# Opening, end and twelve chunks of filling work moved in a one-core encoder block kernel

## The chip, the core and the metric

The kernel runs on one core of one Trainium2 chip. The metric is the device time of one execution in microseconds (us), lower is better. Three executions of the kernel before took 1316.39, 1316.41 and 1317.48 us; their median is 1316.41.

## The reference: one encoder layer

For 1024 tokens of 1024 features (float32) the layer computes:

```
h = RMSNorm(x);  P = h @ w_in -> q_A k_A v_A | q_B k_B v_B | gate_A gate_B
A = 2-D neighbourhood attention, 8 heads of 64, learned bias, QK-norm
B = sliding-window attention (128 tokens to each side), 8 heads, 2 key/value heads, sink, T5 bias
y = sigmoid(gate_A) * (A @ w_branch_a) + sigmoid(gate_B) * (B @ w_branch_b)
x = x + y @ w_out
x = x + (silu(RMSNorm(x) @ w_gate) * (RMSNorm(x) @ w_up)) @ w_down
```

## The kernel before, in words

Every float32 product is made of three fp32r products (high by high, high by low, low by high), so each operand is split into a high and a low half: ScalarE (ACT) casts the high half, VectorE (DVE) subtracts it to get the low one. TensorE (PE) then issues matmuls in groups of three. Here a **chunk** is such a group of three matmuls; one of the gates' product (lines L422 to L424) has 512 columns, one of a projection (L320 to L322) 384.

**Opening.** `first_row` is the first 128x512 piece of the transposed input, and `weights[0].load(0)` loads three strips of 128 columns of `w_in`, the first 256 of 1024 rows (tile `wg_0s`). `load_small` loads a small table `cols` on ACT's queue. SyncE (SP) issues almost all other loads. PE meanwhile does 24 transposes of the identity into a bank that nothing reads (tile `idle`, L529). The first projection then goes through eight steps k, each needing a split strip of weights and a split, scaled piece of the input (`h`); strips 0 and 1 come from `wg_0s`, strips 2 and 3 from the next load, `wg_1s`.

**Attention.** 16 heads in six groups (neighbourhood, window, neighbourhood, window, neighbourhood, neighbourhood) give 128 steps of one 128-query block. In a step PE makes scores `s` (L593, L594); DVE adds the bias and takes the maximum (tile `E`, L599); ACT does the exponential (L605); DVE a reciprocal (L606); GpSimd (POOL) scales `E` (L607). Three steps later PE transposes `E` into `tp` (L617), ACT and DVE split it into `ph` and `pl`; five steps later PE multiplies these by the values into `o` (L651). In names such as `s5_0_3` the numbers are group, head and block.

Between these, PE is given **filling work**: the next group's projection (64 chunks for each of groups 1 to 5), then three gate products of 16 chunks each (`pg`, evacuated to `graw`). How many chunks are done by which step is a list of due chunks (`due`) at marks (`marks`, the step two before a group starts), joined by straight lines (`plan`). Independently of it, a step whose group's projection isn't finished asks for chunks one by one until it is (`while hd["gi"] not in ready`). A projection ends with the layout of its last four token tiles (`tk`, `tq` transposes, then `k1`, `q` by ACT and DVE), which is taken from a list at given chunks: for the last group, after the 7th and the 12th chunk of the first gate product. Sums of input rows for later products (`row_sums`, tiles `ta`, `tb`, `hs`, on DVE and ACT) are tied to the gates' chunks 26 to 33 and 40 to 47.

The order on PE is written out by the program. On DVE, ACT, POOL and SP a scheduler places the instructions of this stage.

**End.** The last product, down-projection, accumulates seven partial products per pair of blocks into four banks; bank Z of the last pair is read by DVE and added to `acc` (L1438), and SP writes `acc` out (L1440).

Of the kernel before, what the change touches and what calls it, by code (L numbers as in the profile page):

```python
# [25 lines left out]
def block_kernel(ctx, tc, x, xt, small, w_in, rpb, t5, w_ba, w_bb, w_out, w_gate, w_up, w_down,  # L26
                 onehot, swmask, namask, out):
    nc = tc.nc
# [13 lines left out]
    def bank(tag, name):  # L42
        return psp.tile([P, 512], F32, tag=tag, name=name, bufs=BANKS[tag])

    def f(ap):
        return ap.bitcast(F32)

    def split(hi, lo, src, eng=None, scale=None):
        if scale is None:
            a = nc.scalar.copy(hi, src)  # L50
            b = (eng or nc.vector).tensor_tensor(lo, src, f(hi), ALU.subtract)  # L51
        else:
            a = nc.scalar.activation(hi, src, AF.Copy, scale=scale)
            b = nc.vector.scalar_tensor_tensor(lo, src, scale, f(hi), op0=ALU.mult, op1=ALU.subtract)
        return a.ins, b.ins
# [9 lines left out]
    def w_stage(name):  # L65
        return wp.tile([P, 1024], F32, tag="wst", name=name + "s", bufs=2)
# [4 lines left out]
    def slot_v(nm, dt=F32):  # L71
        return big.tile([P, T], dt, tag="V", name=nm, bufs=8)
# [14 lines left out]
    def half_cols(h):  # L87
        return slice(h * 512, h * 512 + 512)

    LO, HI = half_cols(0), half_cols(1)  # L90
# [11 lines left out]
    def tok(t):  # L102
        return slice(t * P, (t + 1) * P)
# [60 lines left out]
    def load_small():  # L164
        nc.scalar.dma_start(cols, small)
        nc.vector.tensor_scalar_mul(nsink, nsink, -1.0)
        for b in "ab":
            nc.vector.tensor_scalar_mul(gk[b], gk[b], HD ** 0.5)
# [12 lines left out]
    order = [("na", 0), ("sw", 0), ("na", 1), ("sw", 1), ("na", 2), ("na", 3)]  # L181

    def group_columns(kind, idx):
        if kind == "na":
            return ((128 * idx, 128), (512 + 128 * idx, 128), (1024 + 128 * idx, 128)), 2, 2
        return ((1536 + 256 * idx, 256), (2048 + 64 * idx, 64), (2176 + 64 * idx, 64)), 4, 1

    class GroupWeights:
# [4 lines left out]
            self.ranges = group_columns(*order[gi])[0]  # L193
            self.st, self.his, self.los = [], [], []

        def load(self, u, queues=(nc.sync,) * 3):
            st = (self.spare[u - 2] if self.spare and u > 1 else w_stage(f"wg{self.gi}_{u}"))[:, :768]
            st = st.rearrange("p (k c) -> p k c", k=2)
            c0 = 0
            for queue, (off, w) in zip(queues, self.ranges):  # L200
                queue.dma_start(st[:, :, c0:c0 + w],
                                  w_in[0, u * 256:(u + 1) * 256, off:off + w].rearrange("(k p) c -> p k c", p=P))
                c0 += w
            self.st.append(st)
# [313 lines left out]
    weights = {gi: GroupWeights(gi, spare.get(gi, ())) for gi in range(len(order))}  # L518

    first_row = slot_v("x0_0")[:, :512]  # L520
    weights[0].load(0, (nc.sync, nc.scalar, nc.sync))
    load_small()
    nc.sync.dma_start(first_row, xt[tok(0), LO])
    warm = cst.tile([P, 1], F32, name="warm")
    nc.scalar.activation(warm, mhalf[:, 0:1], AF.Exp)

    idle = bank("o", "idle")
    for i in range(24):
        nc.tensor.transpose(idle[:, tok(i % 4)], ident, ident)  # L529

    with tc.tile_pool(name="at", bufs=1) as ap:
# [175 lines left out]

        due, marks = [], []
        for gi, (kind, _) in enumerate(order):
            due.append(64 * gi + (26 if gi == 0 else 18 if kind == "sw" else 12))  # L710
            marks.append(max(0, sum(8 * group_columns(*z)[1] for z in order[:gi]) - 2))
        n_fill = 64 * (len(order) - 1) + 48
        plan = np.interp(np.arange(1, n + LP + 1), marks + [n + LP], due + [n_fill])
# [44 lines left out]
    def scratch2(nm):  # L758
        return hp.tile([P, 1024], F32, tag="e4", name=nm, bufs=4)
# [9 lines left out]
    def in_turn(*gens):  # L769
        gens = list(gens)  # L770
        while gens:
            gens = [g for g in gens if next(g, gens) is not gens]
# [208 lines left out]
    for n, (d, half) in enumerate(turns):  # L981
# [18 lines left out]
        if half == 0:  # L1000
            p = 2 if d % 2 else 1
# [49 lines left out]
    def prefetch_down(b):  # L1051

        if b > 11:
            return
        k0, n = CHUNKS[b // 4]
        i = b % 4
        st = w_stage(f"wda{b}"), w_stage2(f"wdb{b}")
        src = w_down[0, 2 * k0 * P:2 * (k0 + n) * P, 2 * i * P:2 * (i + 1) * P]
        src = src.rearrange("(j a p) c -> a p j c", a=2, p=P)
        ks = [t[:, :256 * n].rearrange("p (j c) -> p j c", c=256) for t in st]  # L1060
        for a in range(2):
            dma(ks[a], src[a])
        downs[b] = Seven(f"d{b}", [[z[:, :, tok(r)] for z in ks] for r in range(2)], n, mx, sets)
# [342 lines left out]
    for i in range(4, NF, 2):  # L1406
# [6 lines left out]
        for p in ORDER[1:]:  # L1413
# [5 lines left out]
    acc = [big.tile([P, T], F32, tag="H", name=f"acc{m}", bufs=16) if m < 4 else scratch2(f"acc{m}")  # L1419
           for m in range(8)]  # L1420
    for m in range(8):
        dma(acc[m], x1_dram[tok(m), :])
    for ch, (k0, n) in enumerate(CHUNKS):
        for q, p in enumerate(ORDER):
            for j in range(n):
                hi, lo = mv[p][j]
                row = (7 * (k0 + j) + q) * P
                nc.sync.dma_start(f(lo), u_dram[row:row + P, :])
                with tc.issue_after(att["first"]):
                    split(hi, lo, f(lo))  # L1430

        def down(i):
            s = downs[4 * ch + i]
            for p in ORDER:
                s.step(p)
                for z, m, h in {2: ("X00",), 5: ("V01", "V11"), 7: ("Z11",), 3: ("Y01",), 4: ("Z10",)}.get(p, ()):
                    m, c = 2 * i + int(m), half_cols(int(h))
                    nc.vector.tensor_add(acc[m][:, c], s.banks[z], acc[m][:, c])  # L1438
                    if ch == 2 and p != 5:
                        nc.sync.dma_start(out[tok(m), c], acc[m][:, c])  # L1440
                if p == 2:
                    prefetch_down(4 * ch + i + 2)
                yield

        for i in (0, 2):
            in_turn(down(i), down(i + 1))
# [74 lines left out]
```

## Time and profile before

| | |
|---|---|
| median of three executions | 1316.41 us |
| the profiled execution | 1315.88 us |
| its span (first to last recorded instruction) | 1313.9 us |
| PE busy | 1303.5 us (99%) |
| DVE busy | 1018.0 us (77%) |
| ACT busy | 695.3 us (53%) |
| granted TensorE clock | 1.0 of full speed |

The span is the stretch that the records cover; about 2.0 us of the execution lie around it. PE is nearly always busy, so a change counts by what it does to PE's few idle stretches, to the stretch ahead of PE's first useful matmul and to the one behind its last.

### The profile page before, as it was taken

To read this page: it belongs to the slowest core of one execution; us is meant where nothing else is said; L and a number is where in the kernel's file an instruction comes from. 1 tells how busy PE (TensorE), PEld (TensorE's weight loads), DVE (VectorE), ACT (ScalarE), POOL (GpSimd) and SP (SyncE) were. 2 spreads that over 40 slices of the span, in tenths; PEclk is the share of its full clock that TensorE was granted. 3 is DMA by queue.
4 is the path that set the end of the run, shared out by engine and by line. 5 is a ranking of instruction groups with operands and counts; after the bars stand their busy time and mean duration, and the time that the engine had idled before them with its cause. 6 is when DMAs were issued, how large, how long until landed. Compare 5 with 4: busy or idle time off the path is not lost.

```text
span 1313.9 us, 19620 instructions
## 1 busy us (share of the span) xinstructions
PE 1303.5 (99%) x6616; PEld 1133.4 (86%) x6616; DVE 1018.0 (77%) x2039; ACT 695.3 (53%) x1459; POOL 182.4 (14%) x322
## 2 busy tenths in 40 slices
PE   9999999999999999999999999999999999999998
PEld 8999999999888788888888888888888888888887
DVE  5678867776687758869999878888777799688765
ACT  6667867776664324636556544443444455363532
POOL 1364645564320000000000000000000000000000
PEclk9999999999999999999999999999999999999999
DMA  9532324241535348757774533233233356672532
GB/s 309 149 89 60 107 66 109 61 134 53 149 117 179 120 151 271 240 179 230 250 238 122 167 105 112 81 104 117 84 106 121 120 172 221 241 248 65 184 121 89
DMA packets 180997, 191.92 MB, mean 146 GB/s; under 512 B 21104, under 2 KB 126576, under 8 KB 180896
## 3 DMA queue, kind: packets, MB, share of 16 engines
q1 hardware_dynamic: 180368, 190.44, 46.3%
q8 instruction: 52, 0.85, 0.3%
q14 instruction: 49, 0.40, 0.1%
q10 hardware_dynamic: 528, 0.23, 0.1%
HBM read 133.19 MB, written 52.37 MB: 141 GB/s over the span
## 4 chain that ended last, share of the span: by engine, by line
PE 85%; DVE 7%; DMA 4%; ACT 2%; issue 1%; SPq 1%; POOL 1%; ACTq 0%; DVEq 0%; POOLq 0%
PE bankZ L825 5%; PE bankZ L826 5%; PE bankZ L827 5%; PE bankY L826 5%; PE bankY L825 5%; PE bankY L827 5%; PE pj L320 4%; PE pj L322 4%; PE pj L321 4%; PE bankX L826 4%; PE bankX L827 4%; PE bankX L825 4%; PE o L651 3%; PE tp L617 3%; PE bankV L826 3%; PE bankV L825 3%
## 5 line engine op out<-in xcount | busy, mean ns | idle before, releaser
L605 ACT ACTIVATE E<-E,nm 128x384 f32<-128x384 f32 (+3 forms) x128 | 75.7, 592 | 47.8 <-DVE nm L599 42.1
L607 POOL TENSOR_SCALAR E<-E,nm 128x384 f32<-128x384 f32 (+1 forms) x128 | 74.3, 581 | 94.6 <-DVE nm L606 71.5
L51 DVE TENSOR_TENSOR pl<-tp,ph 128x384 fp32r<-128x384 f32 (+1 forms) x128 | 66.4, 519 | 17.7 <-ACT ph L50 16.6
L50 ACT CAST ph<-tp 128x384 fp32r<-128x384 f32 (+1 forms) x128 | 57.4, 449 | 21.0 <-PE tp L617 20.2
L50 ACT CAST f<-f 128x512 fp32r<-128x512 f32 x87 | 51.3, 620 | 25.2 <-DMA f<-u_dram 24.4
L51 DVE TENSOR_TENSOR f<-f 128x512 fp32r<-128x512 f32 x87 | 56.3, 682 | 8.7 <-ACT f L50 8.7
L617 PE MATMUL tp<-ident,E 128*128 128x128 f32 x352 | 59.5, 272 | 0.9 <-POOL E L607 0.9
L617 PEld LDWEIGHTS tp<-ident,E 128*128 128x128 f32 x352 | 45.2, 140 | 5.9 <-POOL E L607 1.2
L340 POOL TENSOR_TENSOR ss<-ss,mhalf 128x4 f32<-128x4 f32 (+2 forms) x42 | 49.8, 1185 | 3.2
L651 PE MATMUL o<-pl,v 128*128 128x256 f32 (+2 forms) x160 | 48.6, 304 | 0.4 <-DVE pl L51 0.3
L606 DVE RECIPROCAL nm<-nm 128x1 f32<-128x1 f32 x128 | 20.4, 161 | 35.3 <-ACT E L605 34.0
L1215 POOL TENSOR_TENSOR rs<-rs,mhalf 128x4 f32<-128x4 f32 x2 | 2.8, 1421 | 317.6 <-DVE rs L1214 317.6
L651 PE MATMUL o<-ph,v 128*128 128x256 f32 (+2 forms) x160 | 45.9, 301 | 0.3 <-ACT ph L50 0.3
L593 PE MATMUL s<-k,q 128*128 128x384 f32 (+1 forms) x128 | 46.0, 359 | 0.0
L594 PE MATMUL s<-k,q 128*128 128x384 f32 (+1 forms) x128 | 41.4, 323 | 0.0
L599 DVE CUSTOM_DVE_ANT_0 E<-s,bsw,cols 128x384 f32<-128x384 f32 (+1 forms) x64 | 36.9, 577 | 4.4 <-PE s L594 3.7
L1232 ACT ACTIVATE u<-u 128x512 f32<-128x512 f32 x44 | 27.5, 629 | 19.7 <-DVE u L1231 19.6
L599 DVE CUSTOM_DVE_ANT_0 E<-s,bna 128x384 f32<-128x384 f32 (+1 forms) x64 | 32.9, 516 | 4.4 <-PE s L594 3.8
L825 PE MATMUL bankZ<-f,f_4h 128*128 128x512 f32 x88 | 34.6, 393 | 0.6 <-DVE p L1349 0.6
L1233 DVE TENSOR_TENSOR u<-u,wide_rs 128x512 f32<-128x512 f32 x44 | 30.0, 687 | 6.4 <-ACT u L1232 5.6
L826 PE MATMUL bankV<-f,f_5h 128*128 128x512 f32 x88 | 34.4, 391 | 0.0
L825 PE MATMUL bankV<-f,f_5h 128*128 128x512 f32 x88 | 34.4, 391 | 0.0
(1268 smaller groups left out, 4636.2 us busy)
## 6 DMA issues: line engine op xcount, KB each, us to landing
f<-u_dram SPq DMA_DIRECT2D x77, 256.0 KB
wg_s<-in_w_gate_dram SPq DMA_DIRECT2D x22, 512.0 KB
u_dram<-u SPq DMA_DIRECT2D x33, 256.0 KB
o_dram<-of SPq DMA_DIRECT2D x32, 256.0 KB
o<-o_dram SPq DMA_DIRECT2D x32, 256.0 KB
sg<-g_dram SPq DMA_DIRECT2D x32, 256.0 KB
g_dram<-go SPq DMA_DIRECT2D x24, 256.0 KB
u_dram<-tau SPq DMA_DIRECT2D x22, 256.0 KB
```

The lines of the kernel that those rows point to most:

```text
L50: a = nc.scalar.copy(hi, src)
L51: b = (eng or nc.vector).tensor_tensor(lo, src, f(hi), ALU.subtract)
L320: nc.tensor.matmul(ps[:, :384], lh, his[k][:, :384], start=(k == 0), stop=False)
L321: nc.tensor.matmul(ps[:, :384], lh, los[k][:, :384], start=False, stop=False)
L599: att["bound"] = nc.vector.tensor_tensor_reduce(E[:, :n], s[:, :n], hd["bias"](qb), -1.0, sk if sw else 1e30, ALU.add, ALU.min, nm[:, 0:1] ...
L605: nc.scalar.activation(E[:, :m], E[:, :m], AF.Exp, bias=nm[:, 0:1], scale=-1.0, accum_out=nm[:, 1:2])
L607: nc.gpsimd.tensor_scalar(E[:, :n], E[:, :n], nm[:, 1:2], 1.0, op0=ALU.mult, op1=ALU.mult)
L617: nc.tensor.transpose(tp[:, tok(j)], hd["E"][qq][:, ko:ko + P], ident)
L651: nc.tensor.matmul(hd["O"][half][:, (a - half * 4) * P:(z + 1 - half * 4) * P], v[:, kb].rearrange("p a e -> p (a e)"), pp[:, (a - q0) * P ...
L825: nc.tensor.matmul(ps, hi[:, tok(j)], bh, start=first, stop=False, skip_group_check=True)
L826: nc.tensor.matmul(ps, hi[:, tok(j)], bl, start=False, stop=False, skip_group_check=True)
L827: nc.tensor.matmul(ps, lo[:, tok(j)], bh, start=False, stop=end, skip_group_check=True)
```

## The change

The diff has three edits. In the opening, `first_row` goes first and on ACT's queue, all three strips of `wg_0s` go on SP's queue, and two of the 24 idle transposes are dropped. In the plan, the last group's due chunk at its mark falls from 332 to 320, so that the twelve chunks between are planned after the mark. At the end, `acc`'s left half of the last block is added into bank Z by DVE before the last partial product, and the finished bank is copied out in two halves of 256 columns, by DVE and by ACT, each written out from a queue of its own.

```diff
-        def load(self, u, queues=(nc.sync,) * 3):
+        def load(self, u):
...
-            for queue, (off, w) in zip(queues, self.ranges):
-                queue.dma_start(st[:, :, c0:c0 + w],
+            for off, w in self.ranges:
+                nc.sync.dma_start(st[:, :, c0:c0 + w],
...
     first_row = slot_v("x0_0")[:, :512]
-    weights[0].load(0, (nc.sync, nc.scalar, nc.sync))
+    nc.scalar.dma_start(first_row, xt[tok(0), LO])
+    weights[0].load(0)
     load_small()
-    nc.sync.dma_start(first_row, xt[tok(0), LO])
...
-    for i in range(24):
+    for i in range(22):
         nc.tensor.transpose(idle[:, tok(i % 4)], ident, ident)
...
-            due.append(64 * gi + (26 if gi == 0 else 18 if kind == "sw" else 12))
+            due.append(64 * gi + (26 if gi == 0 else 18 if kind == "sw" else 0 if gi == len(order) - 1 else 12))
...
                 for z, m, h in {2: ("X00",), 5: ("V01", "V11"), 7: ("Z11",), 3: ("Y01",), 4: ("Z10",)}.get(p, ()):
                     m, c = 2 * i + int(m), half_cols(int(h))
+                    if (ch, i, p) == (2, 3, 4):
+
+                        for copy, queue, o in ((nc.vector.tensor_copy, nc.sync, 0), (nc.scalar.copy, nc.scalar, 256)):
+                            part = acc[m][:, o:o + 256]
+                            copy(part, s.banks[z][:, o:o + 256])
+                            queue.dma_start(out[tok(m), o:o + 256], part)
+                        continue
                     nc.vector.tensor_add(acc[m][:, c], s.banks[z], acc[m][:, c])
                     if ch == 2 and p != 5:
                         nc.sync.dma_start(out[tok(m), c], acc[m][:, c])
+                    if (ch, i, p) == (2, 3, 7):
+                        nc.vector.tensor_add(s.banks[z], s.banks[z], acc[m][:, LO])
```

**PE at the first steps of the last group.** Before, from the scores `s5_0_0` on:

```order
L593 MATMUL s5_0_0_4992<-k15_0_4020,q5_0_4016 128x256 [waits DVE_49]
L594 MATMUL s5_0_0_4992<-k25_0_4022,q5_0_4016 128x256 [waits DMAHW3_49,DMAHW2_49]
L651 MATMUL o4_1_0_4951<-ph4_1_3_4963,v4_1_3000 128x256 [waits Activation_49]
L651 MATMUL o4_1_0_4951<-pl4_1_3_4964,v4_1_3000 128x256 [waits DVE_49]
L422 MATMUL pg1_1_0_5006<-h0_0_88,wg11_0h_4887 128x512
L423 MATMUL pg1_1_0_5006<-h0_0_88,wg11_0h_4887 128x512
L424 MATMUL pg1_1_0_5006<-h0_0_88,wg11_0l_4888 128x512
L617 MATMUL tp4_1_5_5014<-ident_74,E4_1_4_4830 128x128 [waits PE_49]
L617 MATMUL tp4_1_5_5014<-ident_74,E4_1_5_4898 128x128
L617 MATMUL tp4_1_5_5014<-ident_74,E4_1_6_4940 128x128 [waits Pool_49]
L593 MATMUL s5_0_1_5022<-k15_0_4020,q5_0_4016 128x384
```

Now, from the end of the layout transposes on:

```order
L294 MATMUL tq5_4_0_4969<-ident_74,qn5_7_4841 128x128
L593 MATMUL s5_0_0_4978<-k15_0_4018,q5_0_4014 128x256
L594 MATMUL s5_0_0_4978<-k25_0_4020,q5_0_4014 128x256 [waits DMAHW3_49,DMAHW2_49]
L651 MATMUL o4_1_0_4869<-ph4_1_3_4878,v4_1_2998 128x256
L651 MATMUL o4_1_0_4869<-pl4_1_3_4879,v4_1_2998 128x256
L617 MATMUL tp4_1_5_4989<-ident_74,E4_1_4_4765 128x128
L617 MATMUL tp4_1_5_4989<-ident_74,E4_1_5_4806 128x128
L617 MATMUL tp4_1_5_4989<-ident_74,E4_1_6_4832 128x128 [waits Pool_49]
L593 MATMUL s5_0_1_4997<-k15_0_4018,q5_0_4014 128x384
L594 MATMUL s5_0_1_4997<-k25_0_4020,q5_0_4014 128x384
L651 MATMUL o4_1_0_4869<-ph4_1_4_4903,v4_1_2998 128x128
```

Seven of the twelve chunks (`pg0_1_0`, `pg0_1_1`) and the layout transposes `tk5_4`, `tq5_4_0` stand directly ahead of `s5_0_0`, where the step asks for them; the steps `s5_0_0`, `s5_0_1` and `s5_0_2` have no chunk, from `s5_0_3` on each has about two.

**DVE at the same place.** Before:

```order
L599 ISA E5_0_0_4995,nm5_0_0_4996<-s5_0_0_4992,bna6_4689 128x256 [waits DMAHW6_49,PE_49,Pool_49]
L599 ISA nm5_0_0_4996 128x1
L599 ISA E5_0_1_5025,nm5_0_1_5026<-s5_0_1_5022,bna6_4689 128x384 [waits DVE_49,PE_49]
L599 ISA nm5_0_1_5026 128x1
L51 TENSOR_TENSOR pl4_1_5_5019<-tp4_1_5_5014,ph4_1_5_5018 128x384 [waits DVE_49,Activation_49]
L606 RECIPROCAL nm5_0_0_4996<-nm5_0_0_4996 128x1 [waits Activation_49]
L599 ISA E5_0_2_5056,nm5_0_2_5057<-s5_0_2_5053,bna6_4689 128x384 [waits DVE_49,PE_49]
```

Now:

```order
L599 ISA E5_0_0_4981,nm5_0_0_4982<-s5_0_0_4978,bna6_4651 128x256 [waits DMAHW7_49,PE_49,Pool_49]
L599 ISA nm5_0_0_4982 128x1
L273 SCALAR_TENSOR_TENSOR q5_0_4014<-tq5_4_0_4969,cols_81,q5_0_4014 64x512 [waits Activation_49]
L599 ISA E5_0_1_5000,nm5_0_1_5001<-s5_0_1_4997,bna6_4651 128x384 [waits PE_49]
L599 ISA nm5_0_1_5001 128x1
L606 RECIPROCAL nm5_0_0_4982<-nm5_0_0_4982 128x1 [waits Activation_49]
L51 TENSOR_TENSOR pl4_1_5_4994<-tp4_1_5_4989,ph4_1_5_4993 128x384 [waits Activation_49]
L599 ISA E5_0_2_5025,nm5_0_2_5026<-s5_0_2_5022,bna6_4651 128x384 [waits DVE_49,PE_49]
L599 ISA nm5_0_2_5026 128x1
L273 SCALAR_TENSOR_TENSOR q5_1_4015<-tq5_4_0_4969,cols_81,q5_1_4015 64x512 [waits Activation_49]
L51 TENSOR_TENSOR pl4_1_6_5019<-tp4_1_6_5014,ph4_1_6_5018 128x384 [waits Activation_49]
L606 RECIPROCAL nm5_0_1_5001<-nm5_0_1_5001 128x1 [waits Activation_49]
```

The two layout instructions `q5_0` and `q5_1` now stand among the first steps' softmax; before they were done some seven steps earlier.

**DVE and ACT at the end.** DVE, before:

```order
L1438 TENSOR_TENSOR acc7_11792<-bankZ1_6645,acc7_11792 128x512 [waits DVE_49,PE_49]
L1438 TENSOR_TENSOR acc4_11789<-bankY0_6639,acc4_11789 128x512 [waits PE_49]
L1438 TENSOR_TENSOR acc6_11791<-bankY1_6643,acc6_11791 128x512 [waits PE_49]
L1438 TENSOR_TENSOR acc5_11790<-bankZ0_6641,acc5_11790 128x512 [waits PE_49]
L1438 TENSOR_TENSOR acc7_11792<-bankZ1_6645,acc7_11792 128x512 [waits PE_49]
```

DVE now:

```order
L1445 TENSOR_TENSOR acc7_11790<-bankZ1_6643,acc7_11790 128x512 [waits DVE_49,PE_49]
L1449 TENSOR_TENSOR bankZ1_6643<-bankZ1_6643,acc7_11790 128x512
L1445 TENSOR_TENSOR acc4_11787<-bankY0_6637,acc4_11787 128x512 [waits PE_49]
L1445 TENSOR_TENSOR acc6_11789<-bankY1_6641,acc6_11789 128x512 [waits PE_49]
L1445 TENSOR_TENSOR acc5_11788<-bankZ0_6639,acc5_11788 128x512 [waits PE_49]
L1442 COPY acc7_11790<-bankZ1_6643 128x256 [waits DVE_49,PE_49]
```

ACT now (the last two of its work are new):

```order
L50 CAST d10_4h_13501<-wdb10_13192 128x384 [waits PE_49,Activation_49]
L829 COPY bankZ0_6639<-bankY0_6637 128x512 [waits PE_49]
L50 CAST d11_4h_13516<-wdb11_13215 128x384 [waits PE_49,Activation_49]
L829 COPY bankZ1_6643<-bankY1_6641 128x512 [waits PE_49]
L1442 COPY acc7_11790<-bankZ1_6643 128x256 [waits DVE_49]
L1443 DMA out_0_dram<-acc7_11790 128x256 [waits DMAHW6_49,Activation_49]
```

ACT's copy waits on DVE's semaphore alone: the value it waits for is the one that DVE's copy of the other half sets.

## Rows read from the trace of the kernel before

**Rows 1.** The page's busy times.

```profile
PE 1303.5 (99%) x6616; PEld 1133.4 (86%) x6616; DVE 1018.0 (77%) x2039; ACT 695.3 (53%) x1459; POOL 182.4 (14%) x322
```

**Rows 2.** Waits of PE, whole span: us in total, times, longest.

```profile
PE tp L617 <- POOL E L607: 0.9, 1, 0.9
PE tq L294 <- DVE k L288: 0.6, 1, 0.6
```

**Rows 3.** Timeline of the opening: start us, us, instruction, idle before.

```profile
0.72 0.49 ACTq L201 DMA_DIRECT2D wg_0s<-in_w_in_dram  x1
...
1.73 0.47 SPq L523 DMA_DIRECT2D x<-in_xt_dram  x1
...
4.32 0.51 ACT L50 CAST wg_0h<-wg_0s 128x384 fp32r<-128x384 f32 x1 [1.05 <-DMA wg_0s<-in_w_in_dram]
...
6.20 0.72 ACT L53 ACTIVATE h<-x,cols 128x512 fp32r<-128x512 f32 x1 [1.36 <-DMA x<-in_xt_dram]
...
6.97 0.45 PE L320 MATMUL pj<-wg_0h,h 128*128 128x384 f32 x1 [0.19 <-ACT h L53]
...
10.80 0.51 ACT L50 CAST wg_2h<-wg_1s 128x384 fp32r<-128x384 f32 x1 [2.86 <-DMA wg_1s<-in_w_in_dram]
...
11.99 0.45 PE L320 MATMUL pj<-wg_2h,h 128*128 128x384 f32 x1
```

**Rows 4.** Windows of the opening: busy by engine, clock, DMA share, GB/s.

```profile
4.00:6.97 2.97, 2.78 (x14) 2.48 (x13) 0.86 (x5) 1.29 (x3) 0.00 (x0) 1.00 0.86 290
6.97:12.00 5.03, 4.72 (x25) 4.07 (x25) 2.45 (x5) 2.17 (x5) 0.00 (x0) 1.00 1.02 322
```

**Rows 5.** Windows in the last two groups' steps, same columns.

```profile
340.00:360.00 20.00, 20.00 (x116) 17.52 (x115) 13.96 (x42) 12.53 (x32) 6.39 (x11) 1.00 0.56 175
360.00:380.00 20.00, 18.96 (x108) 16.06 (x107) 17.51 (x49) 14.17 (x37) 7.01 (x12) 1.00 0.51 159
```

**Rows 6.** PE's timeline, one step of the last group.

```profile
349.25 0.42 PE L593 MATMUL s<-k,q 128*128 128x384 f32 x1
...
349.68 0.40 PE L422 MATMUL pg<-h,wg_0h 128*128 128x512 f32 x1
...
350.38 0.22 PE L651 MATMUL o<-ph,v 128*128 128x128 f32 x1
...
350.55 0.52 PE L617 MATMUL tp<-ident,E 128*128 128x128 f32 x3
350.82 0.48 PE L422 MATMUL pg<-h,wg_0h 128*128 128x512 f32 x1
```

**Rows 7.** Groups from 280 to 385 us: count, busy us, mean ns.

```profile
L51 DVE TENSOR_TENSOR pl<-tp,ph 128x384 fp32r<-128x384 f32 x30 | 16.6, 553 | 5.9 <-ACT ph L50 5.8
...
L599 DVE CUSTOM_DVE_ANT_0 E<-s,bna 128x384 f32<-128x384 f32 x24 | 13.1, 549 | 1.1 <-PE s L594 0.9
...
L606 DVE RECIPROCAL nm<-nm 128x1 f32<-128x1 f32 x38 | 5.9, 160 | 10.5 <-ACT E L605 10.0
...
L273 DVE SCALAR_TENSOR_TENSOR q<-tq,cols,q 64x512 fp32r<-64x512 f32 x6 | 4.5, 750 | 1.4 <-ACT q L272 1.3
...
L51 DVE TENSOR_TENSOR pl<-tp,ph 128x256 fp32r<-128x256 f32 x10 | 4.2, 418 | 1.8 <-ACT ph L50 1.7
...
L50 ACT CAST ph<-tp 128x256 fp32r<-128x256 f32 x10 | 3.7, 368 | 5.1 <-PE tp L617 5.1
```

**Rows 8.** Timeline at PE's longest attention wait.

```profile
376.72 1.15 POOL L607 TENSOR_SCALAR E<-E,nm 128x384 f32<-128x384 f32 x2 [3.14 <-DVE nm L606]
...
377.36 0.33 PE L617 MATMUL tp<-ident,E 128*128 128x128 f32 x1 [0.94 <-POOL E L607]
```

**Rows 9.** Timeline of the end.

```profile
1309.82 0.39 PE L827 MATMUL bankZ<-f,d_4l 128*128 128x512 f32 x1
1310.25 0.69 DVE L1438 TENSOR_TENSOR acc<-bankZ,acc 128x512 f32<-128x512 f32 x1 [1.35 <-PE bankZ L827]
1310.97 0.33 SPq L1440 DMA_DIRECT2D out_dram<-acc  x1
```

## Prediction

> **What bounds the kernel now.** I read the busy times first: PE works 1303.5 us of a span of 1313.9, DVE 77%, ACT 53% [rows 1]. The three edits take no matmul away that anything needs: the projections, scores, gate chunks and the last product have as many as before, only two idle transposes fall out. So a gain can lie only where PE stands still, some 10 us in all, and a loss arises where PE is made to stand still. The second view was the list of PE's waits. Two of them lie near the change: 0.9 us on POOL's scaling of `E`, once, and 0.6 us on DVE's layout of a key tile, once [rows 2]. Then I read the timelines and windows of the three places that the diff touches. In the opening, from 4.00 to 6.97 us, PE is doing only idle work, and the transfer engines are 0.86 busy; from there to 12.00 they are 1.02 busy, that is, full, at 322 GB/s, while PE is busy 4.72 of 5.03 us [rows 3, 4]. In the last group's steps PE is first completely busy with DVE at 13.96 of 20 us, then idle for 1.04 of 20 us with DVE at 17.51 of 20 [rows 5]: that second stretch holds the row sums, and DVE is what limits it. At the end one addition and one output DMA stand behind PE's last matmul.
>
> All terms below are changes against the profiled execution, 1315.88 us. It is 0.53 us under the median of the runs, 1316.41; I add that at the end.
>
> **Opening: 0 (from -0.6 to +0.4).** Now the first projection matmul starts at 6.97, held by ACT's `h`, 0.72 us at 6.20, which waited 1.36 us for the piece of x [rows 3]. That piece was issued at 1.73, behind three other issues; moved ahead on ACT's queue it would be issued a microsecond earlier, where the strip of `wg_0s` is issued now, at 0.72. ACT is then limited by the cast of `wg_0h`, 0.51 us at 4.32, whose strips now all go in a row on SP and land somewhat later, so I let `h` start some 0.5 us earlier, and PE with it; dropping two idle transposes frees PE in time for that. But PE's ninth chunk (25 matmuls lie between 6.97 and 12.00 [rows 4]) needs strip 2, which belongs to the next load: its cast starts at 10.80 after ACT waited 2.86 us for the data, and PE takes it up at 11.99 [rows 3]. Until then the transfer engines are full, and the bytes ahead of `wg_1s` are the same in another order [rows 4]. PE would thus begin 0.5 us sooner and stand 0.5 us longer before 11.99. The ends of the bound are the whole 0.6 us kept, and a `wg_1s` that comes 0.4 us later because ACT's queue now carries x, or because its own load slips behind the other strips on SP. I take 0, as the row with share 1.02 is the nearest.
>
> The Trainium skill, "DMA: Bandwidth & Descriptors", section "Issuing engines are not separate DMA queues", says that loads started by different engines run on the same 16 DMA engines and interleave, so another issuer saves only the issue time. By that rule the second queue brings nothing once these are full, as the share of 1.02 shows they are [rows 4]; if queues were separate, the 0.6 us would be kept.
>
> **Wait for the key layout: -0.3 (from -0.6 to 0).** The one wait of 0.6 us [rows 2] falls in the fourth group's steps, where the plan now asks for 52 chunks over 16 steps instead of 64, 3.25 a step instead of 4. DVE and PE shift against each other there; nothing says that the wait must go or stay, so I take half.
>
> **First steps of the last group: +1.7 (from 0 to +2.5).** The due number 320 does not move all twelve chunks behind the mark. The last group's layout hangs on the 7th and the 12th chunk of the first gate product, which are numbers 327 and 332, and the step asks for chunks until its group is ready. So seven chunks and eight layout transposes are issued in one block in front of `s5_0_0`, and `s5_0_0` to `s5_0_2` are left without any. What PE does from the start of `s5_0_0` until `tp5_0_0`, by the order: four pairs of scores, one of them at 256 columns; twelve `o` matmuls of 3072 columns in all; eight transposes. One pair of scores takes 0.43 us from start to start, a matmul of 512 columns about 0.235 (three in 0.70), three transposes 0.27 [rows 6]. That is 0.29 + 3 x 0.43 = 1.58, 6 x 0.235 = 1.41, 8 x 0.09 = 0.72: about 3.7 us. Before, the chunks of those steps, 0.70 us each, made it some 6 us.
>
> On DVE, `tp5_0_0` needs the reciprocal of `nm5_0_1`, behind which POOL scales `E5_0_1`. Ahead of that reciprocal stand `E5_0_0`, `q5_0`, `E5_0_1`, a reciprocal, `pl4_1_5`, `E5_0_2`, `q5_1` and `pl4_1_6`. With 0.55 for each `E` and `pl`, 0.75 for each `q`, 0.16 for a reciprocal [rows 7]: 3 x 0.55 + 2 x 0.75 + 2 x 0.55 + 2 x 0.16 = 4.57 us. With 0.3 until the first scores are there and 0.58 for POOL (two take 1.15 [rows 8]) that is 5.4 us against PE's 3.7: PE stands 1.7 us, on `pl` or on `tp5_0_0`. The lower end, 0, is a DVE that takes no part of its work in this stretch: it was 13.96 of 20 us busy before [rows 5], and the seven chunks, 4.9 us in a row, let it empty its queue, but `q5_0` and `q5_1` wait for a transpose that comes after those chunks, so they can't be done in that time. The upper end adds 0.8 for two handoffs with ACT, whose part (0.37 for 256 columns of `ph` [rows 7]) stands ahead of each `pl`. I take the sum of the rows, 1.7.
>
> **Row sums in the later steps: -0.6 (from -1.0 to +0.7).** From 360 to 380 PE is idle for 1.04 us, of which 0.94 is one wait for `E` at 377.36 [rows 5, 8]. With the chunks left over, steps there have about two chunks instead of one and a half, 0.35 us more of PE's work to a step of some 2.1 us, under the same DVE work per step. Most of the wait should go, up to all of it. The other end is that the row sums, tied to chunk numbers, come in steps that are already crowded: one addition of 0.7 us [rows 9] too many.
>
> **End: +0.1 (from -0.35 to +0.3).** Today DVE adds for 0.69 us from 1310.25, and SP issues the output at 1310.97 [rows 9]. The copy of 256 columns should cost 0.42 on DVE, as `pl` of 256 [rows 7], 0.27 less. Side by side with ACT's, 0.37, this would bring some 0.3. But by the order ACT's copy waits for the value that DVE's copy sets: 0.42 + 0.05 + 0.37 = 0.84 against 0.69, so the last output is issued 0.15 later; it carries half the bytes, for which I take off 0.05. The new addition into bank Z, 0.69 on DVE, lies before the last partial product, where DVE waited 1.35 us [rows 9]; if that cover were gone it would cost up to 0.7.
>
> The Trainium skill, "PSUM — Partial Sum Buffer", section "PSUM bank collisions raise a hardware error", says that two engines may not touch the same bank and quadrant in the same cycle, whichever columns, so that accesses have to be ordered. That is a reason for the wait in the order; by it the end is 0.1 late, and without it 0.3 early. No run here shows a collision.
>
> **Sum.** 0 - 0.3 + 1.7 - 0.6 + 0.1 = +0.9 on 1315.88, hence 1316.8, and with the 0.53 of the median **1317.3 us**.
>
> **Rivals.**
> - *Faster, the block of chunks is covered.* For: in the stretch from 340 DVE has 6 us of 20 free [rows 5], and POOL and the exponential run ahead. Against: the two `q` can't start before the block ends. Then the first steps cost 0.2, the wait in the row sums goes whole (-1.0), the key layout's too (-0.6), and opening and end give -0.6 and -0.3: -2.3 on the median, 1314.1 with everything kept, about 1314.8 if the opening is swallowed.
> - *Slower, DVE's queue in the last group.* The first steps leave DVE behind, and with two chunks a step the row sums' and the evacuations' instructions come closer. In DVE's order `pl5_1_1`, on which PE's `o5_1_0` hangs, has three splits or sums of up to 0.69 [rows 9] and about four of 0.4 to 0.55 [rows 7] ahead of it, some 3.7 us. If DVE is more than a microsecond late when it comes to them, PE pays 2 to 3 us: 1317.3 + 2.3 = 1319.6. For: DVE was 17.51 of 20 busy there [rows 5]. Against: PE's steps there become longer.
> - *The change does nothing that counts.* The seven chunks are asked for before the first step anyway, the five others fall into steps in which DVE keeps up, opening and end are hidden: 1316.4.
>
> **How the numbers follow.** My forecast 0.55, the change that does nothing 0.2, faster 0.15, slower 0.1. The range of the likeliest alone is 1316.0 to 1318.3. For 8 in 10 I take 1314.8 to 1318.9: it holds the forecast, the empty case, and part of both others. A measurement of this kernel can tell about 0.2% from no change, 2.6 us here, so 1313.8 to 1319.0 count as the same. Only the whole of the faster case with more than its best ends reaches below that (0.05), and nearly all of the slower case lies above it (0.09); 0.86 is left for no change.
>
> **What would show it.** Right: PE idle between 1 and 2.5 us from `s5_0_0` to `tp5_0_0`, put down to DVE's `pl` or POOL's `E`; the cast of `wg_2h` still near 10.8 though PE begins before 6.97; ACT's copy at the end starting only when DVE's ends; the wait of 0.94 gone or under 0.4. Wrong: PE without a gap after the block of seven chunks; a cast of `wg_2h` earlier by as much as the first matmul; two copies overlapping; or a wait of over 1 us on `pl` in the second head of the last group.

## The result, and the profile after

The changed kernel took 1318.73 us (median of 21 runs) against 1316.53 for the kernel before (21 runs): a ratio of 1.0014 with a 95% interval of [1.0008, 1.0020], or 1.8 us slower (1.1 to 2.6). The forecast was 0.9 us slower, 1317.3 us, with a range of 1314.8 to 1318.9; the median lies 0.2 us under the upper end of that range. It had also said that a difference under 0.2% counts as no change, and 1.0014 is under it, though the interval is clear of 1. The profiled execution of the changed kernel took 1318.22 us, its span is 1316.3.

The busy times of the page after, as [rows 1] of before:

```profile
PE 1303.6 (99%) x6614; PEld 1132.7 (86%) x6614; DVE 1019.9 (77%) x2040; ACT 694.8 (53%) x1460; POOL 181.0 (14%) x322
```

PE's work is the same to 0.1 us, though two transposes fewer; the 2.4 us by which the span is longer are time in which PE stands. The list of PE's waits after, over the whole span (us in all, times, longest), answers to [rows 2]:

```profile
PE o L651 <- DVE pl L51: 1.5, 4, 0.5
PE o L651 <- ACT ph L50: 1.2, 2, 0.6
...
PE tp L617 <- POOL E L607: 0.3, 1, 0.3
PE tq L294 <- DVE k L288: 0.3, 1, 0.3
```

The waits on POOL and on the key layout shrank, as forecast; new ones stand in front of `o`, on DVE's `pl` and on ACT's `ph`. Not all of these two lines is the change's: 0.51 us of `pl` and 0.59 of `ph` lie at 277 us, ahead of the place where the plans part. Before, 0.27 and 0.29 us lay there, and e3, which leaves the plan alone, has 1.05 of `ph`; so this part differs from run to run. The same holds for a wait of 0.68 us at 492, for ACT's copy between two banks, where e1 has 0.95. The windows of the same stretches as [rows 5], and the next:

```profile
340.00:360.00 20.00, 18.98 (x107) 15.95 (x107) 13.84 (x39) 12.94 (x31) 5.92 (x9) 1.00 0.44 123
360.00:380.00 20.00, 19.76 (x109) 16.77 (x108) 15.57 (x41) 12.65 (x31) 4.18 (x7) 1.00 0.44 131
380.00:400.00 20.00, 19.11 (x94) 15.52 (x93) 11.96 (x24) 8.03 (x17) 1.06 (x2) 1.00 0.49 146
```

PE was idle 0, 1.04 and 0 us there before (the third window of before has PE busy 20.00 of 20), now 1.02, 0.24 and 0.89. A matmul's record overlaps the next one's start, so idle time understates a delay: the distance from start to start tells more.

**First steps of the last group**, from the timeline after:

```profile
344.80 0.68 ACT L272 ACTIVATE q<-tq,cols 64x512 fp32r<-64x512 f32 x1 [0.99 <-PE tq L294]
...
345.60 0.74 DVE L273 SCALAR_TENSOR_TENSOR q<-tq,cols,q 64x512 fp32r<-64x512 f32 x1
...
346.46 0.33 PE L594 MATMUL s<-k,q 128*128 128x384 f32 x1
346.47 0.59 ACT L630 COPY of<-o 128x512 f32<-128x512 f32 x1
...
347.11 0.33 PE L651 MATMUL o<-ph,v 128*128 128x128 f32 x1 [0.32 <-ACT of L630]
...
347.98 0.76 DVE L273 SCALAR_TENSOR_TENSOR q<-tq,cols,q 64x512 fp32r<-64x512 f32 x1
...
348.60 0.33 PE L651 MATMUL o<-ph,v 128*128 128x384 f32 x1
...
349.38 0.45 PE L651 MATMUL o<-pl,v 128*128 128x384 f32 x1 [0.44 <-DVE pl L51]
...
349.66 0.27 PE L617 MATMUL tp<-ident,E 128*128 128x128 f32 x1
...
350.20 0.33 PE L617 MATMUL tp<-ident,E 128*128 128x128 f32 x1 [0.27 <-POOL E L607]
```

Three idle stretches: 0.32, 0.44 and 0.27 us, 1.03 in all. By starts, matmuls that otherwise follow after 0.18, 0.18 and 0.09 us came after 0.65, 0.78 and 0.54: 0.47 + 0.60 + 0.45 = 1.5 us. The first hangs on ACT: the copy of the finished `o` out of the only bank for `o` came late, behind the q cast, an exponential and a cast of `ph`. The second hangs on DVE, where `q` at 347.98 stands ahead of the `pl`. Before, DVE did these two `q` at 344.00 and 345.51, ahead of `s5_0_0` at 347.82: two steps earlier, and not some seven, as the section on the change has it.

**The last steps**, ACT, SP and PE after:

```profile
373.44 1.09 SPq L637 DMA_DIRECT2D o_dram<-of  x2
...
374.63 0.53 SPq L450 DMA_DIRECT2D g_dram<-graw  x1
...
375.26 1.20 SPq L97 DMA_DIRECT2D xe<-in_xt_dram  x1
...
376.56 0.41 SPq L97 DMA_DIRECT2D xo<-in_xt_dram  x1
...
377.06 0.39 SPq L865 DMA_DIRECT2D ga3s<-in_w_in_dram  x1
...
382.64 0.72 ACT L497 ACTIVATE g22h<-xo,cols 128x512 f32<-128x512 f32 x1 [3.21 <-DMA xo<-in_xt_dram]
...
383.26 0.40 PE L424 MATMUL pg<-h,wg_0l 128*128 128x512 f32 x1
...
383.76 0.46 ACT L50 CAST ph<-tp 128x384 fp32r<-128x384 f32 x1
...
384.27 0.33 PE L651 MATMUL o<-ph,v 128*128 128x128 f32 x1 [0.62 <-ACT ph L50]
...
384.87 0.33 PE L651 MATMUL o<-pl,v 128*128 128x128 f32 x1 [0.27 <-DVE pl L51]
```

SP before, same stretch:

```profile
371.11 0.33 SPq L450 DMA_DIRECT2D g_dram<-graw  x1
371.53 0.38 SPq L97 DMA_DIRECT2D xe<-in_xt_dram  x1
372.00 0.41 SPq L97 DMA_DIRECT2D xo<-in_xt_dram  x1
...
372.81 0.38 SPq L865 DMA_DIRECT2D ga3s<-in_w_in_dram  x1
375.28 1.10 SPq L637 DMA_DIRECT2D o_dram<-of  x2
```

Before, the loads of the second pair of input rows (`xe`, `xo`) stood behind a gate's output (`g_dram`) and ahead of the output of a head (`o_dram`); now they stand behind both, and `xo` is issued 4.6 us later. SP itself stood 7.6 us, up to 373.44, for ACT, whose copy `of` the store `o_dram` writes out, with the loads behind it. ACT reaches the first operation on them (`g22h`) when they haven't landed, stands 3.21 us, and the cast `ph5_1_4` that PE needs stands behind it. By starts PE loses some 0.8 us at 384.27 (1.01 instead of 0.23) and 0.5 at 384.87 (0.60 instead of 0.07).

**The opening**, as [rows 3]:

```profile
0.72 0.46 ACTq L521 DMA_DIRECT2D x<-in_xt_dram  x1
...
5.94 0.51 ACT L50 CAST wg_0h<-wg_0s 128x384 fp32r<-128x384 f32 x1 [2.71 <-DMA wg_0s<-in_w_in_dram]
6.36 0.72 ACT L53 ACTIVATE h<-x,cols 128x512 fp32r<-128x512 f32 x1
...
7.12 0.44 PE L320 MATMUL pj<-wg_0h,h 128*128 128x384 f32 x1 [0.97 <-ACT h L53]
...
10.62 0.51 ACT L50 CAST wg_2h<-wg_1s 128x384 fp32r<-128x384 f32 x1 [2.52 <-DMA wg_1s<-in_w_in_dram]
...
11.84 0.42 PE L320 MATMUL pj<-wg_2h,h 128*128 128x384 f32 x1
```

x no longer comes last: ACT casts `wg_0h` at 5.94 instead of 4.32 and goes on to `h` at once. In this profile PE begins at 7.12, not sooner, and reaches strip 2 at 11.84 instead of 11.99. One profile says little here. Over all runs below, the ten profiles with the new opening have PE begin at 6.75 to 7.22, the four with the old one (before, e2, e3, e4) at 6.97 to 7.60. Strip 2 is reached at 11.6 to 11.8 in seven of the ten and at 13.2 to 13.3 in three (e7, e8, e13; see the last section), with the old opening at 12.0 to 12.3.

**The end**, as [rows 9]:

```profile
1311.86 0.39 PE L827 MATMUL bankZ<-f,d_4l 128*128 128x512 f32 x1
1312.29 0.43 DVE L1442 COPY acc<-bankZ 128x256 f32<-128x256 f32 x1 [1.35 <-PE bankZ L827]
1312.74 0.33 SPq L1443 DMA_DIRECT2D out_dram<-acc  x1
1312.75 0.37 ACT L1442 COPY acc<-bankZ 128x256 f32<-128x256 f32 x1 [15.95 <-DVE acc L1442]
1313.15 0.37 ACTq L1443 DMA_DIRECT2D out_dram<-acc  x1
```

ACT's copy begins when DVE's has ended; the last output is issued 1.29 us after PE's last matmul starts, before it was 1.15.

### The profile page after: what moved, and what is told of

It reads as the page before. It is cut to its first block, busy times and chain, and to the rows that moved or that the text cites. A ratio compares the mean times of both kernels' runs of the same rounds, so it can differ in the third digit from the quotient of the medians.

```text
span 1316.3 us, 19621 instructions
## 1 busy us (share of the span) xinstructions
PE 1303.6 (99%) x6614; PEld 1132.7 (86%) x6614; DVE 1019.9 (77%) x2040; ACT 694.8 (53%) x1460; POOL 181.0 (14%) x322
## 4 chain that ended last, share of the span: by engine, by line
PE 89%; DVE 4%; DMA 3%; ACT 1%; issue 1%; POOL 1%; SPq 0%; ACTq 0%; POOLq 0%; DVEq 0%
PE bankZ L825 6%; PE bankZ L826 6%; PE bankZ L827 6%; PE bankY L825 6%; PE bankY L826 6%; PE bankY L827 6%; PE bankX L826 4%; PE bankX L825 4%; PE bankX L827 4%; PE pj L320 4%; PE pj L322 4%; PE pj L321 4%; PE bankV L825 3%; PE bankV L826 3%; PE bankV L827 3%; PE o L651 3%
## 5 line engine op out<-in xcount | busy, mean ns | idle before, releaser
L825 PE MATMUL bankV<-f,f_5h 128*128 128x512 f32 x88 | 34.4, 391 | 0.0
L825 PE MATMUL bankY<-f,f_6h 128*128 128x512 f32 x88 | 34.4, 390 | 0.0
```

The costliest lines, as they stand in the source:

```text
L825: nc.tensor.matmul(ps, hi[:, tok(j)], bh, start=first, stop=False, skip_group_check=True)
```

## The experiments

Each was run beside the kernel before on the same chip; ratios are to it, with 95% intervals. "Idle" is PE's idle time from 340 to 400 us by the windows view. "Stretch" is the time on PE from the first scores of step 94, counted from 0, two steps ahead of group 4 (287.25 us before, 287.11 after), to the first matmul behind the last gate product (L825 `bankX`, 401.02 and 402.82). In it every kernel here has the same matmuls and transposes, in another order, so it is a measure by starts of what the plan costs. The three profiles with the plan of before (before, e1, e3) give 113.8 to 114.2, so a difference under some 0.4 us of one profile says little.

| run | ratio | interval | idle | stretch |
|---|---|---|---|---|
| before | 1 | – | 1.04 | 113.8 |
| the changed kernel | 1.0014 | [1.0008, 1.0020] | 2.15 | 115.7 |
| e1_opening | 1.0002 | [0.9993, 1.0011] | 1.04 | 114.0 |
| e2_due | 1.0014 | [1.0005, 1.0022] | 2.54 | 115.9 |
| e3_end | 0.9997 | [0.9987, 1.0007] | 1.14 | 114.2 |
| e4_due18 | 1.0019 | [1.0010, 1.0029] | 1.70 | 115.2 |
| e5_cover | 1.0005 | [0.9996, 1.0013] | 2.26 | 115.3 |
| e6_late | 1.0011 | [1.0002, 1.0021] | 2.37 | 115.5 |
| e7_noqlow | 1.0006 | [0.9998, 1.0015] | 2.20 | 115.4 |
| e8_both | 1.0003 | [0.9994, 1.0012] | 2.53 | 115.3 |
| e9_loads | 0.9999 | [0.9990, 1.0008] | 1.27 | 114.3 |
| e11_pops | 1.0000 | [0.9990, 1.0010] | 1.31 | 114.3 |
| e12_best | 0.9980 | [0.9970, 0.9990] | 0.44 | 113.0 |
| e13_due12 | 0.9994 | [0.9984, 1.0003] | 1.01 | 113.8 |

**The three edits one by one.** The opening alone, on the kernel before, with the edit as in the change:

> The opening's edit alone on the kernel before (first piece of x on ScalarE's queue, three strips on SyncE's, 22 idle transposes). Theory: PE's first projection matmul is no earlier than 6.97 us (about 7.1, as in the changed kernel, since the strips land later), but the cast of wg_2h comes 0.1 to 0.2 us earlier than 10.80, so the whole is 0.0 to 0.3 us faster than before. Rival (the prediction's 0): no measurable change and wg_2h at 10.8. Second rival: the later start of PE, 0.15 us, stays, and the kernel is 0.1 to 0.3 us slower.

No measurable change: the interval goes from 0.9 us faster to 1.4 slower and can't tell the three cases apart. That PE begins no earlier than 6.97 was wrong: in this profile it began at 6.75 us and reached strip 2 at 11.70.

The due number alone:

```diff
-  ... else 18 if kind == "sw" else 12))
+  ... else 18 if kind == "sw" else 0 if gi == len(order) - 1 else 12))
```

> The due number of the last group alone (332 to 320) on the kernel before. Theory: it carries nearly all of the change's loss: PE stands about 1.5 us between the scores s5_0_1 and the transpose tp5_0_0, and again 1 to 1.7 us at o5_1_0 around 377 to 385 us, where ScalarE waits about 3 us for a load of input rows (xo) in front of the ph that PE needs; the wait of 0.94 us for E at 377.36 goes. The sum: 1.3 to 2.2 us slower than before. Rival: the loss sits in the end and in chance, and this kernel is within 0.5 us of before.

As expected: the whole loss of the change, 1.8 us (0.7 to 2.9), with the same waits at the same places; the stretch is 2.1 us longer than before, in the changed kernel 1.9. Its list of PE's waits from 340 to 400 us:

```profile
PE o L651 <- ACT ph L50: 1.0, 1, 1.0
PE o L651 <- DVE pl L51: 0.9, 3, 0.4
PE o L651 <- ACT of L630: 0.3, 1, 0.3
PE tp L617 <- POOL E L607: 0.3, 1, 0.3
```

The end alone:

> The end's edit alone on the kernel before. Theory: ScalarE's copy starts only when VectorE's ends, the last output is issued 1.29 us after PE's last matmul starts instead of 1.15, and the stretch from that matmul to the span's end grows from 4.1 to about 4.4 us: 0.2 to 0.4 us slower than before. Rival: half the bytes in the last transfer give the 0.14 us back, 0.0 to 0.2 us slower; or the two copies lie side by side, 0.3 us faster.

No measurable change. ACT's copy began at 1311.39, when DVE's ended, and from the last matmul's start (1310.51) to the span's end (1314.5) it took 4.0 us, against 4.1 before and 4.4 in the changed kernel. Of the ten profiles with the new end six took 4.0 us and four 4.4 to 4.8 (changed, e6, e7, e9); the four with the old end took 4.1 each. So the new end costs nothing in some runs and 0.3 to 0.7 us in others; why is open. The ratio, from 1.7 us faster to 0.9 slower, doesn't tell my theory from the rivals.

**More chunks ahead instead of fewer**, on the kernel before:

```diff
-  ... else 18 if kind == "sw" else 12))
+  ... else 18 if kind == "sw" else 18 if gi == len(order) - 1 else 12))
```

> The due number of the last group raised instead (332 to 338) on the kernel before: six chunks more ahead of the last group's first step. Theory (DVE and ACT queues in the last group set the waits, and which chunk meets which step decides them): the first steps keep a chunk each and PE has no gap there; the steps from 360 us on have 30 chunks in 23 steps, 1.3 a step, so that PE outruns VectorE more: the waits at 366 to 378 us grow from 1.5 to 2 or 2.5 us, 0 to 1 us slower than before. Rival: fewer chunks late means earlier loads and row sums with more time, 0.5 to 1 us faster.

Slower by 2.5 us (1.3 to 3.8), more than I had said. PE's longest wait there is for POOL's `E`, 1.4 us, where before it was 0.9: with fewer chunks late, PE runs ahead of the softmax. The wait for the key layout grew too, from 0.6 to 1.0 us at 313.12 (with 320 it is 0.3). The stretch holds 1.4 us of the 2.5; the rest is not found. So both directions from 332 lose, by different waits.

**Where the first steps lose.** Chunks put into the bare steps of the changed kernel:

```diff
+            if 112 <= g < 117:
+                fill(done_chunks[1] + 1)
             fill((before + plan[g]) / 2)
```

> The changed kernel with one chunk given to PE in each of the first five steps of the last group (they come out of the later steps; same chunks in all). Theory (in the bare steps PE outruns VectorE, which has the two q layouts and the splits to do): the three gaps at o4_1_1, o4_1_1 and tp5_0_0 (1.0 us by the gap list of the due change alone, 1.5 with what hides in the pipeline) go, the waits at 377 and 384 us stay; 1.0 to 1.5 us less than the changed kernel, so 0.3 to 0.9 us over before. Rival: DVE's backlog is not worked off but handed on, and the same wait comes back in the steps behind, within 0.3 us of the changed kernel (about 1.8 us over before).

The three gaps nearly went (0.07 us of the first is left), but a new one of 0.53 us came at `tp5_0_2` two steps behind, for DVE's `pl`, and the wait at 384 us stayed, at 1.2. Some of the gain was handed on, as the rival had it: the stretch is only 0.4 us shorter than in the changed kernel. The ratio's interval allows either size.

The q's low halves taken from DVE:

```diff
+                if gi == len(order) - 1 and s0 == 4:
+                    return lambda: nc.gpsimd.memset(f(lo_of), 0.0)
                 return lambda: nc.vector.scalar_tensor_tensor(lo_of, ...
```

> The changed kernel without the low halves of the last group's q for the tokens from 512 on: VectorE's two instructions of 0.75 us are left out and GpSimd writes zeros much earlier, so the scores of the last four blocks lose their small correction. Theory of the prediction (the two q in VectorE's queue make up most of its lateness, 1.5 of 5.4 us against PE's 3.7): the gaps at o4_1_1 and tp5_0_0 shrink from 1.0 us in all to under 0.3, 0.8 to 1.4 us less than the changed kernel. Rival: ScalarE sets the pace there (exponentials, two q casts of 0.68 us and a copy of o in its queue), the gaps stay at 0.6 us or more and little is gained.

By the trace the rival holds: with DVE free there, PE stands on ACT in one piece, and the stretch is 0.3 us shorter than in the changed kernel. The ratio is lower by 0.0008, 1.1 us, which the theory had said, but the two intervals overlap. From its timeline:

```profile
345.30 1.38 ACT L272 ACTIVATE q<-tq,cols 64x512 fp32r<-64x512 f32 x2 [0.99 <-PE tq L296]
...
347.70 0.59 ACT L632 COPY of<-o 128x512 f32<-128x512 f32 x1
...
348.35 0.33 PE L653 MATMUL o<-ph,v 128*128 128x128 f32 x1 [1.06 <-ACT of L632]
```

The two q casts, 1.38 us in a row, push the copy of `o` back, and the gap is as long as the three were (1.06 against 1.03). In the changed kernel the second cast stood behind that copy (347.08 against 346.47); here the scheduler put it ahead, so e7 differs from the changed kernel in ACT's order too, and doesn't show what DVE's part alone is worth. It shows that the layout so close ahead of the steps loads both engines: freeing DVE is not enough.

So the layout itself was moved ahead by some chunks, with the due number as in the change:

```diff
-                if (half, k) in ((0, 6), (1, 3), (2, 1)):
+                if (half, k) in ((0, 2), (0, 6)):
                     pop(pending)
```

> The changed kernel with the last group's two layouts after the 3rd and the 7th chunk of the first gate product instead of the 7th and the 12th: the last group is ready after 327 chunks, the block in front of s5_0_0 has two or three chunks instead of seven, and the first steps keep one or two chunks each. Theory (the loss in the first steps comes from the block, which puts q layouts on VectorE and ScalarE right into the first steps, and from the bare steps): the three gaps there (1.0 us) fall under 0.3, 0.8 to 1.5 us less than the changed kernel; the waits at 377 and 384 us stay. Rival: the q layouts still fall into the first steps and the gaps stay, or come back as waits for the layout itself (tq, tk).

The gaps fell from 1.03 to 0.20 us, the ratio to 1.0000 and the stretch by 1.4 us; the waits at 375 and 382 us stayed (0.24, 0.60, 0.27), as the theory said. The rival's first half came true as well: DVE does the two `q` at 341.61 and 344.12, still behind `s5_0_0` at 340.53. But the steps have chunks again: from `s5_0_1` the next two scores come after 2.4 and 3.2 us (341.34, 343.70, 346.94), in the changed kernel after 0.9 and 2.0 (345.32, 346.20, 348.17). So it is the layout together with the bare steps that makes PE stand.

**Where the last steps lose.** ACT's `g22h` held behind a later cast:

```diff
-                    with tc.issue_after(att["bound"]):
+                    with tc.issue_after(att["bound"]), tc.issue_after(att["ph" if at_step > 39 else "bound"]):
```

(`att["ph"]` is the last cast `ph`.)

> The changed kernel with ScalarE's first operation on the second pair of input rows (g22h from xo) put behind the cast ph5_1_5 in ScalarE's order, five instructions later, so that it no longer waits for its load with the cast ph5_1_4 behind it. Theory: the wait of ScalarE of 3.2 us at 382.6 goes, and with it PE's gaps at o5_1_0 around 384 us (0.9 us by the gap list); 0.9 to 1.3 us less than the changed kernel, 0.5 to 0.9 over before. Rival: the next cast on ScalarE, of weights that land still later (ga3s), takes the place of the wait, and less than 0.3 us is gained; or VectorE's late splits hold PE there anyway.

The rival holds: the next cast on ACT waits for the load behind, 1.96 us, and `ph5_1_5` and a copy of `o` stand behind it. PE stood 1.11 us at 385.67 for that copy; by ratio 0.4 us is gained, by the stretch 0.2.

```profile
383.00 0.62 ACT L50 CAST g_1h<-ga3s 128x512 fp32r<-128x512 f32 x1 [1.96 <-DMA ga3s<-in_w_in_dram]
...
384.42 0.72 ACT L497 ACTIVATE g22h<-xo,cols 128x512 f32<-128x512 f32 x1
```

With the chunks of e5 added:

> The changed kernel with both mends: a chunk in each of the first five steps, and ScalarE's g22h of the second pair behind ph5_1_5. If the two gaps are separate causes their gains add: 1.9 to 2.6 us less than the changed kernel, from 0.1 over before to 0.8 us under it, since the wait of 0.94 us for E of the kernel before is gone too. Rival: VectorE is the bound of the whole last group (its work is the same), and what is taken away at one place comes back at another: under 1 us gained, still about 1 us over before.

1.0003 and a stretch of 115.3: a gain over the changed kernel, but no more than e5 alone shows. PE stood 1.7 us at `o5_1_1` for the copy of `o` behind the same cast, which now waited 2.55.

Then the loads were asked for earlier as well, on top of e6:

```diff
-                if at_step == 32:
+                if at_step == 28:
                     load_pair(1, slot_v, dma)
```

> The changed kernel with g22h of the second pair behind ph5_1_5 as in e6, and the loads of that pair (xe, xo) asked for four chunks earlier, so that on SyncE's queue they stand ahead of the two output stores of o_dram. Theory (ScalarE's wait is made by the order on SyncE's queue, where the loads xe, xo and ga3s now stand behind o_dram and graw): ScalarE waits under 0.5 us for xo and ga3s together, PE's gap of 0.9 to 1.1 us at 384 to 386 us goes, the excess of the stretch from 330 to 395 us falls from 6.8 to about 6; 0.7 to 1.2 us less than e6. Rival: the transfers themselves are the limit (1.5 MB of loads in some 7 us), the wait moves to another cast and under 0.3 us is gained.

SP's queue in this run:

```profile
365.75 0.32 SPq L97 DMA_DIRECT2D xe<-in_xt_dram  x1
366.18 0.41 SPq L97 DMA_DIRECT2D xo<-in_xt_dram  x1
372.95 1.09 SPq L637 DMA_DIRECT2D o_dram<-of  x2
```

ACT's waits for loads are gone from 370 to 392 us, and so are PE's at 384 to 386; 1.0011 went to 0.9999, and the stretch fell by 1.2 us. It was the order on SP's queue: ahead of `o_dram` the loads are issued some 10 us earlier than in the changed kernel, because they no longer stand behind SP's wait for ACT. The ratios of e6 and e9 overlap in their intervals; the waits and the stretch are what shows it.

**Both mended** (e11 and e9 together), and the same with the due number back at 332:

> The changed kernel with both: layouts after the 3rd and 7th chunk, and the second pair's loads earlier with its g22h behind ph5_1_5. If both losses of the changed kernel are mended and the wait of 0.94 us for E of the kernel before stays away, it is 0.3 to 1.0 us under the kernel before. Rival: VectorE and ScalarE together are the bound of the last group, some 5 us of excess between 330 and 395 us stay in whatever form, and it is the same as before within 0.5 us.

> The kernel with both mends (layouts after the 3rd and 7th chunk, second pair's loads earlier, its g22h held behind a later cast), but with the due number of the last group back at 332: is it the later chunks that are faster there, or only the mends? Theory: the kernel before has no loss that the mends touch (its first steps have no gap and ScalarE waits for no load), and its wait of 0.94 us for E near 377 us goes only when the chunks come later; so this kernel is within 0.6 us of the kernel before, and the due number gives 1.3 to 2.5 us once its two losses are mended. Rival: the mends help the kernel before as much, and this one is 1.3 us or more faster than before; then the due number is worth nothing.

```profile
340.00:360.00 20.00, 19.80 (x114) 17.11 (x113) 13.45 (x40) 12.07 (x30) 6.45 (x10) 1.00 0.49 142
360.00:380.00 20.00, 19.76 (x109) 16.91 (x108) 15.52 (x43) 13.77 (x34) 4.79 (x8) 1.00 0.49 147
380.00:400.00 20.00, 20.00 (x98) 16.70 (x97) 13.65 (x23) 7.73 (x15) 0.00 (x0) 1.00 0.55 168
```

With both mends (the windows are e12's) PE is idle 0.44 us in 60, and the kernel is faster than before by 2.6 us (1.3 to 3.9), more than I expected, and than the 0.6 us of idle time that it saves against the kernel before. It beats both kernels. The stretch is 2.7 us shorter than in the changed kernel, which is what e11 (1.4) and e9 (1.4) save one by one: the two losses are separate, and their gains add. Against the kernel before it is 0.8 us shorter; where the rest of the 2.6 comes from is open. With 332 the wait for `E`, 0.9 us, is back, the ratio is 0.9994, not told from before, and the stretch is that of before, 113.8. So the mends alone give nothing that shows there, as the theory said, and in the stretch the due number is worth 0.8 us once they are in; by the ratios it is 1.8, with intervals that overlap.

## Why the prediction was right, and where it was wrong

The direction and one of the two places of the loss were right, and the median lies in the range (1314.8 to 1318.9), 0.2 us from its upper end. The forecast of 0.9 us was half of what was measured, and most of the difference lies in one step, which put the second place down as a gain.

- **Opening, 0: right in sum, partly by luck.** I had PE begin 0.5 us sooner and stand 0.5 longer ahead of strip 2. In the profile of the change it began at 7.12, since the strips landed 1.6 us later; whether that comes from sharing the transfer engines with x or from the third strip standing last on SP's queue, no run separates. Over all profiles PE begins about 0.4 us sooner (7.0 against 7.4 in the mean) and hardly stands in front of strip 2: seven of the ten keep the gain, and three lose 1.1 us by slower matmuls, which I had not seen coming. In the mean strip 2 is reached at 12.2 with either opening. Of the Trainium skill's "DMA: Bandwidth & Descriptors", section "Issuing engines are not separate DMA queues" (transfers issued by different engines interleave on the same 16), the traces agree as far as they go: x no longer comes last, `wg_0s` lands some 1.4 us later in the mean of the profiles, and e1 shows no gain.
- **Key layout, -0.3: right.** PE's wait fell from 0.6 to 0.3 us. That half was a choice between two ends and not derived; the wait follows the due number in every run (1.0 us with 338, 0.6 with 332, 0.3 with 320).
- **First steps, +1.7: right in size, half right in cause.** 1.03 us of idle time, some 1.5 by starts, and e11 takes 1.4 us off the stretch (1.8 by the ratios). From `s5_0_0` at 344.52 to the last transpose of `tp5_0_0` at 350.20 it took 5.7 us, where DVE's chain gave 5.4; PE's own part was 4.2 instead of 3.7. I had put all of it on DVE's queue; the first of the three gaps hangs on ACT's copy of `o`, and e7 shows that with DVE free ACT makes PE stand as long.
- **Row sums, -0.6: this step failed.** "Most of the wait should go" held for the wait for `E`, 0.94 us, which went. But I saw late chunks only as longer steps for PE and as DVE's additions, at most 0.7 us. The chunk numbers also set when loads are asked for: `xe`, `xo` and `ga3s` fell behind a head's output on SP's queue, ACT waited 3.21 us with PE's cast behind it, and PE stood 0.62 and 0.27 us at 384, beside 0.24 at 377. That is 1.13 us against the 1.04 of [rows 5], and in e2 1.5: +0.1 to +0.5 by idle time. By the stretch, 1.9 us longer, +0.7 is left beside the first steps' 1.5 and the key layout's -0.3. So the term is +0.1 to +0.7 instead of -0.6; with it the forecast's own sum would have been 1.6 to 2.2, around the 1.8 measured. e9 shows the cause.
- **End, +0.1: right in the order, not shown in size.** The order on the bank is as read: ACT's copy starts at 1312.75, when DVE's ends at 1312.72. That is what the Trainium skill, "PSUM — Partial Sum Buffer", section "PSUM bank collisions raise a hardware error", asks for: accesses of two engines to one bank are to be ordered. The last output is issued 0.14 us later, as worked out. From PE's last matmul to the span's end the new order takes 4.0 us in six profiles and 4.4 to 4.8 in four, the old one 4.1, so the 0.14 us can't be told from this scatter.
- **The rivals.** The slower one named a wait that came, DVE's queue ahead of `pl5_1_1`, but PE waited there 0.24 us at 377.21, not 2 to 3; the longer wait near it, at 384, hangs on ACT and a load, which no rival had. The rival "covered" did not occur. "Does nothing" is refuted by the interval of the change and by e2.

## What to carry to other kernels

When filling work is shifted by its count, list everything that is tied to the count: loads asked for at a chunk, layouts that a later stage needs, copies that free a bank. Look in the order of each in-order queue for what then stands in front of what the critical engine needs; a load that is issued late on one queue can stop an engine that has work for PE behind it. A mend that only moves the waiting instruction finds the next one that waits for the same transfers; the load's place in its queue had to be moved.

## What the runs showed of the hardware that was not expected

The same program part does not begin at the same time in each run: with the opening of the kernel before, PE's first projection matmul came at 6.97, 7.40 and 7.60 us in three kernels (before, e2, e3), and with the new opening at 7.12, 6.75 and 6.96 (changed, e1, e12). What varies is the landing of the piece that comes last: the cast of `wg_0h` starts at 4.32, 4.33 and 4.31 in the first three, where x comes last, and at 5.94, 5.57 and 5.77 in the others, where the strips do. So 0.2 us in one profile of the opening says nothing.

In three of the ten profiles with the new opening (e7, e8, e13) PE's first projection matmuls came 0.32 us apart up to about 11 us, instead of 0.17, and strip 2 was reached at 13.2 to 13.3 instead of 11.6 to 11.8. In e7 the granted clock of 8 to 11 us reads 0.50, the lower of TensorE's two levels, 1.2 GHz; in e8 and e13 the clock reads 1.00 at the same pace. Ahead of it PE had stood 1.42, 0.62 and 0.77 us behind the idle transposes; but the other seven stood 0.4 to 1.3 us, and e3, with the old opening, 1.80, and kept the full pace. What decides is not shown, nor whether the old opening, with four profiles, is free of it.

And three loads of 512 KB, issued within 1.8 us behind 768 KB of outputs, took until 382.64 for the second, 6.1 us after its issue; before, issued at 372.00, it had landed when ACT came to it at 376.72.
